# Two first output pairs run together, seven products each, with operand splits in an interleaved queue

## The chip, the core and the metric

The kernel runs on one core of a Trainium2 chip. The metric is the device time of one execution in microseconds. The core has five engines that work side by side, each on a queue of its own in a fixed order: TensorE (PE, with its weight loads PEld), VectorE (DVE), ScalarE (ACT), GpSimd (POOL) and SyncE (SP), which here issues the DMAs. An instruction whose semaphore has not come yet holds up all that stands behind it on its engine.

## The reference

A single decoder layer on 2048 rows of 1024 numbers, in float32. Cut to what matters here:

```python
def mixer_layer(h, norm_g, w_in, conv_w, ret_norm_g, w_out, pos):
    hn = rms_norm(h, norm_g)
    proj = jnp.einsum('bld,de->ble', hn, w_in)
    cx, cb, cc, cg, q, k, v, rg = jnp.split(proj, N_PROJ, axis=-1)
    conv_out = short_conv_branch(cx, cb, cc, conv_w) * jax.nn.silu(cg)
    ...
    ret = head_group_norm(retention_chunkwise(qf, kf, vf), ret_norm_g)
    ret_out = ret.astype(h.dtype) * jax.nn.silu(rg)
    mixed = jnp.concatenate([conv_out, ret_out], axis=-1)
    return h + jnp.einsum('ble,ed->bld', mixed, w_out)
# then: h = rms_norm(h, final_g), and the 2048 rows after the 16 meta rows are returned
```

The change lies in the last projection, `mixed @ w_out` (2048x1024 by 1024x1024), the addition of x and the last norm.

## The kernel before

**A product in three matmuls.** To multiply float32 numbers in a faster format, each operand tile of 128x512 is split into a high part (a cast on ScalarE, tiles `wh`, `mh`) and a low part (source minus high part, on VectorE, tiles `wl`, `ml`), line 112 and 113 of `split`. Three matmuls (low by high, high by low, high by high) then make one product of 128x128 by 128x512.

**Seven products for eight.** A big product is cut into 2x2 blocks. `quad` (matmuls at L241) forms the four result blocks from seven block products, after sums of blocks on both sides: Winograd's scheme. Each block product is 4 tiles by 3 matmuls, 12 in all. `stationary` makes the sums on the side of the weights (the tiles `ra` and `sa`, four sums on GpSimd per quad) and splits seven times, through a ring of three buffers (`RING`): a split into a buffer waits until the product that used it three steps earlier has ended. The moving side is split once and used by many quads. Its seven operands `m[0]` to `m[6]` lie in fixed tiles `mh00` to `mh63` (operand, then tile 0 to 3), with one buffer each, so that operand i of a new matrix can be split only after the last product of the old matrix with operand i. `quad_plain` (L298) makes the same four blocks from eight products without any sums; it needs a moving block 7 (in the tiles of operand 4), and its split weights (four) lie in the tiles of operand 3.

**Order of work.** The input projections and the two kinds of mixer heads come first. Their last piece is a convolution group of two quads. Then come eight output pairs; a pair is two row tiles of 128 rows. The matrix w_out is the moving side: its blocks come by DMA as tiles `w`, its sums, which were made earlier and stored in `sums_w`, as tiles `t`, except for eight tiles that are held in SBUF (`held`). The rows of `mixed` are the weights (`ra`). Before the change, `moving` splits the four blocks, pair 0 runs plainly while the sums are being split, and pairs 1 to 7 run as quads. After a pair's product, `take` adds the bank in PSUM, the copy of another bank (`tc`) and x (`yo`): one addition on GpSimd (for pair 1 on VectorE) and one on VectorE, which reads PSUM; then comes the square sum on ScalarE and a multiplication by `final_g` (`z`, GpSimd), and at the end the scaling by the row's factor.

**What sets the order.** The program is written as a flow of tiles. A scheduler puts the instructions of each engine into a fixed order, from the order in which they are written and its own estimate of their lengths; `tc.issue_after(i)` queues what is traced under it behind instruction i on i's engine.

Of the kernel before, what the change touches and what calls it, by code (L numbers as in the profile page):

```python
# [1 line left out]

# [6 lines left out]
F32 = mybir.dt.float32  # L9
# [69 lines left out]
def hybrid_trunk(ctx: ExitStack, tc: tile.TileContext, t, out: bass.AP, chunk_decay):  # L79
# [21 lines left out]
    def gen(name="g"):  # L101
        return sb.tile([P, HB + 16], F32, name=name, tag="g", bufs=GEN)[:, : 2 + HB]
# [1 line left out]
    def brief(name="b"):  # L104
        return sb.tile([P, HB + 128], F32, name=name, tag="b", bufs=BRIEF)[:, :HB]

    lowered, third, fifth = [None], [None], [None]

    def split(hi, lo, src, scale=None, eng=nc.vector):

        if scale is None:
            nc.scalar.copy(out=hi, in_=src)  # L112
            lowered[0] = eng.tensor_tensor(out=lo, in0=src, in1=hi.bitcast(F32), op=ALU.subtract)  # L113
            return
        nc.scalar.mul(hi, src, scale)
        nc.vector.scalar_tensor_tensor(  # L116
            out=lo, in0=src, scalar=scale, in1=hi.bitcast(F32), op0=ALU.mult, op1=ALU.subtract
        )

    def add(eng, out, a, b):  # L120
        eng.tensor_tensor(out=out, in0=a, in1=b, op=ALU.add)  # L121

    def sub(eng, out, a, b):
        eng.tensor_tensor(out=out, in0=a, in1=b, op=ALU.subtract)  # L124
# [6 lines left out]
            tiles.append(a)  # L131
        return tiles

    summed = [None]

    powered, powers = [], []

    def stationary(blocks):

        a11, a12, a21, a22 = blocks  # L140
        s1 = sb.tile([P, HB], F32, name="sa", tag="ra", bufs=RAW)

        def parts(src):
            hi = sb.tile([P, HB], F32R, name="wh", tag="wh", bufs=RING)
            lo = sb.tile([P, HB], F32R, name="wl", tag="wl", bufs=RING)
            split(hi, lo, src)
            return hi, lo

        w = [parts(a11), parts(a12)]
# [4 lines left out]
        summed[0] = nc.gpsimd.tensor_tensor(out=a12, in0=a12, in1=a11, op=ALU.subtract)  # L154
        w.append(parts(a11))
        third[0] = lowered[0]
        w += [parts(a) for a in (s1, a21)]
        fifth[0] = lowered[0]
        return w + [parts(a) for a in (a12, a22)]

    def operand(i, kt):
        slot = B12 if i == 7 else i
# [9 lines left out]
    def moving(load, scale=None, after={}):  # L172


        m = [[] for _ in range(8)]
        blocks = []
        for j in range(2):
            for half in range(2):
                for kt in range(KH):
                    k = half * KH + kt  # L180
                    blocks.append(load(k, j))
                    parts(m, BLOCK[half][j], kt, blocks[-1], scale(k) if scale else None)
                    after.get((j, k), lambda: None)()
        return m, blocks

    def block_sums(b11, b12, b22, b21, t1, t3, f, g, eng=nc.vector):

# [24 lines left out]

    loaded = [None]

    def prepared(m, src, ns, held={}):

        for n in ns:
            for kt in range(KH):
                a = held.get((n, kt))
                if a is None:  # L220
                    a = gen("t")[:, :HB]
                    loaded[0] = nc.sync.dma_start(a, src[n, kt])
                parts(m, SUMS[n], kt, a)
# [6 lines left out]
    def quad(w, m, take, steps=()):  # L230


        steps = iter(steps)

        def product(i, bank, first):
            (wh, wl) = w[i]
            for kt in range(KH):
                ks = slice(kt * P, (kt + 1) * P)
                mh, ml = m[i][kt]
                for n, (a, b) in enumerate(((wl, mh), (wh, ml), (wh, mh))):  # L240
                    nc.tensor.matmul(  # L241
                        bank, a[:, ks], b, start=first and kt == 0 and n == 0, stop=kt == KH - 1 and n == 2,
                        skip_group_check=not first,
                    )
# [29 lines left out]
        take(1, 0, xb, None)  # L274

    def plain_part(n, load, slot):
        a = sb.tile([P, HB], F32, name="ra", tag="ra", bufs=RAW)
# [256 lines left out]
    def group_plain(g, m, f, meta, first, between, ahead):  # L534
# [28 lines left out]
        cs = []  # L563

        def complete():
            with tc.issue_after(third[0].ins):
# [311 lines left out]
            nc.gpsimd.tensor_copy(out=state[h], in_=states[-1])  # L878
        return blocks

    def output(pair, m, final_g):
        d = mixed[pair // 2]
        loads = [
            lambda a, i=i, k=k: nc.sync.dma_start(a.rearrange("p (k c) -> p k c", k=KH), d[pair % 2, i, k])
# [6 lines left out]
        for i in range(2):  # L891
            for j in range(2):
                y = gen("yo")[:, :HB]
                row = (2 * pair + i) * P
                nc.sync.dma_start(y, x[row : row + P, j * HB : (j + 1) * HB])
                ys[i][j] = y
        last = [None]
        squares = []

# [4 lines left out]
        def take(i, j, pp, c):  # L904
            y = ys[i][j]
            if c is not None:

                with tc.issue_after(fifth[0].ins) if pair == 1 and i + j == 0 else nullcontext():
                    add(nc.vector if pair == 1 else nc.gpsimd, y, y, c)
            junk = sb.tile([P, HB], F32, name="rot", tag="rot", bufs=1)  # L910

            cut = 2 if c is None and pair == SEQ // (2 * P) - 1 else 1
            for n in range(cut):
                cs = slice(n * HB // cut, (n + 1) * HB // cut)
                last[0] = nc.vector.tensor_tensor(out=y[:, cs], in0=pp[:, cs], in1=y[:, cs], op=ALU.add)  # L915
                at = ss[:, i, 2 * n : 2 * n + 1] if i != j and n else ss[:, i, j : j + 1]
                if pair and i + j == 0:
# [10 lines left out]
        if pair == 0:  # L928
            w = plain_parts(loads)
            prepared(m, sums_w, (1, 3))  # L930
            quad_plain(w, m, take)
            prepared(m, sums_w, (0, 2), held)
        else:
            quad(stationary(load_raw(loads)), m, take, (idle, idle, square))
        for i in range(2):
            tot = small.tile([P, 1], F32, name="tot", tag="tot")
            add(nc.vector, tot, ss[:, i, 0:1], ss[:, i, 1:2])
            if cuts[i] > 1:
                add(nc.vector, tot, tot, ss[:, i, 2:3])
            rs = small.tile([P, 1], F32, name="rf", tag="rf")  # L940
            rsqrt_mean(rs, tot)
            row = (2 * pair + i) * P
            for j in range(2):
                cs = slice(j * HB, (j + 1) * HB)
                y = ys[i][j]
                if i == j:
                    nc.scalar.mul(y, y, rs)
                else:
                    with tc.issue_after(last[0].ins):
                        nc.vector.scalar_tensor_tensor(  # L950
                            out=y, in0=y, scalar=rs, in1=final_g[:, cs], op0=ALU.mult, op1=ALU.mult
                        )
                (nc.scalar if i == j and cuts[i] > 1 else nc.sync).dma_start(out[row : row + P, cs], y)

    nc.scalar.dma_start(gain, t["norm1_g"])

# [180 lines left out]
```

## Time and profile before

| | |
|---|---|
| median of 3 runs | 868.76 us (868.29 to 868.82) |
| the profiled execution | 868.98 us |
| its span, first to last instruction | 867.2 us |
| granted TensorE clock | 0.999 |
| busy in the span: PE, PEld | 855.4 us, 705.0 us |
| busy: DVE, ACT, POOL | 719.6 us, 497.9 us, 392.9 us |
| HBM read, written | 90.91 MB, 25.17 MB |

Busy time on PE counts matmuls that overlap in a pipeline: one is shown with some 390 ns, and the next starts about 227 ns after it. So a stretch is read by the starts of the first and the last matmul. The last product of the convolution group ends at 708.7 us of the span, with plain matmuls of pair 0 ahead of it; pair 1 begins at 726.4 us, and the last matmul ends at 860.

### The profile page before, as it was taken

The numbers are of one execution on the slowest core, as the hardware profiler recorded it, in microseconds if no ns is written. First come the engines' busy times: TensorE is split into PE (matmuls) and PEld (weight loads), VectorE is DVE, ScalarE is ACT, GpSimd is POOL, SyncE is SP. The second block draws the span as 40 slices with busy tenths as digits, with TensorE's granted clock in tenths as the row PEclk, the third lists the DMA queues.
The fourth block names the chain that finished last, engine by engine and source line by source line (L and its number), as shares of the span: only waits on it lengthen the run. The fifth ranks groups of instructions, "written<-read, shape, count | busy, mean of one in ns | idle before, by whom it ended". The sixth has DMA issues, their size and how long they took to land.

```text
span 867.2 us, 12698 instructions
## 1 busy us (share of the span) xinstructions
PE 855.4 (99%) x4216; PEld 705.0 (81%) x4216; DVE 719.6 (83%) x1194; ACT 497.9 (57%) x899; POOL 392.9 (45%) x286
## 2 busy tenths in 40 slices
PE   8999999999999999999999999999999999999996
PEld 5878888888787778788888888888888888888885
DVE  6879988889998977989789898988767799867663
ACT  8676557384754654848375757544333465545553
POOL 0662232323145545452242333354646445678773
PEclk9999999999999999999999999999999999999999
DMA  9723335464656633855263746646122594555441
GB/s 334 222 83 98 74 74 149 120 159 134 158 170 175 214 98 97 300 162 146 62 157 122 153 140 122 206 111 217 48 76 80 170 331 135 169 181 159 159 134 73
DMA packets 127218, 129.51 MB, mean 149 GB/s; under 512 B 58352, under 2 KB 75568, under 8 KB 127152
## 3 DMA queue, kind: packets, MB, share of 16 engines
q1 hardware_dynamic: 126576, 128.30, 50.5%
q8 instruction: 33, 0.54, 0.3%
q10 hardware_dynamic: 576, 0.40, 0.1%
q14 instruction: 33, 0.27, 0.1%
HBM read 90.91 MB, written 25.17 MB: 134 GB/s over the span
## 4 chain that ended last, share of the span: by engine, by line
PE 76%; DVE 6%; issue 2%; ACT 1%; DMA 1%; POOL 0%; SPq 0%; POOLq 0%; DVEq 0%
PE pj L241 64%; PE pj L298 5%; PE ms L840 1%; PE ms L829 1%; PE ms L839 1%; PE ms L816 1%; DVE wl L113 1%; PE ms L464 1%; DMA w<-in_w_out 1%; DVE ml L113 0%; DVE qg L869 0%; DVE ml L116 0%; DVE w L124 0%; DVE u L605 0%; DVE tc L605 0%
## 5 line engine op out<-in xcount | busy, mean ns | idle before, releaser
L241 PE MATMUL pj<-mh,wl 128*128 128x512 f32 x1008 | 396.0, 393 | 1.0 <-DVE wl L113 1.0
L241 PE MATMUL pj<-mh,wh 128*128 128x512 f32 x1008 | 393.1, 390 | 0.0
L241 PE MATMUL pj<-ml,wh 128*128 128x512 f32 x1008 | 392.8, 390 | 0.0
L112 ACT CAST wh<-ra 128x512 fp32r<-128x512 f32 x216 | 134.0, 620 | 233.7 <-PE pj L241 195.9
L113 DVE TENSOR_TENSOR wl<-ra,wh 128x512 fp32r<-128x512 f32 x216 | 191.2, 887 | 41.9 <-ACT wh L112 40.9
L241 PEld LDWEIGHTS pj<-mh,wl 128*128 128x128 f32 x1008 | 189.3, 188 | 42.7 <-issue 2.0
L241 PEld LDWEIGHTS pj<-mh,wh 128*128 128x128 f32 x1008 | 189.3, 188 | 39.4
L241 PEld LDWEIGHTS pj<-ml,wh 128*128 128x128 f32 x1008 | 189.3, 188 | 38.2
L121 POOL TENSOR_TENSOR sa<-ra 128x512 f32<-128x512 f32 x36 | 53.1, 1475 | 109.3 <-DVE wl L113 44.5
L124 POOL TENSOR_TENSOR ra<-sa,ra 128x512 f32<-128x512 f32 x36 | 51.6, 1434 | 83.2 <-DVE wl L113 75.2
L124 POOL TENSOR_TENSOR ra<-ra 128x512 f32<-128x512 f32 x36 | 58.0, 1611 | 57.7 <-PE ms L464 48.4
L154 POOL TENSOR_TENSOR ra<-ra 128x512 f32<-128x512 f32 x36 | 61.2, 1701 | 46.6 <-issue 35.2
L248 ACT COPY tc<-pj 128x512 f32<-128x512 f32 x108 | 62.7, 580 | 0.1
L298 PE MATMUL pj<-mh,mh 128*128 128x512 f32 x128 | 50.6, 397 | 2.0 <-ACT mh L1017 1.4
L298 PE MATMUL pj<-mh,ml 128*128 128x512 f32 x128 | 50.1, 391 | 0.6 <-DVE ml L113 0.6
L298 PE MATMUL pj<-ml,mh 128*128 128x512 f32 x128 | 48.1, 393 | 0.0
L852 POOL TENSOR_TENSOR rp<-rs,neg_half 128x4 f32<-128x4 f32 x16 | 19.4, 1213 | 45.9 <-DVE rs L121 45.7
L915 DVE TENSOR_TENSOR yo<-pj,yo 128x512 f32<-128x512 f32 (+1 forms) x33 | 22.0, 671 | 17.2 <-PE pj L241 8.5
L926 POOL TENSOR_TENSOR z<-yo,final_g 128x512 f32<-128x512 f32 x16 | 26.8, 1674 | 18.5 <-DVE yo L915 18.5
L605 POOL TENSOR_TENSOR c<-c,rr 128x512 f32<-128x512 f32 x14 | 24.5, 1747 | 20.8 <-DVE c L646 12.7
L605 POOL TENSOR_TENSOR c<-c,tc 128x512 f32<-128x512 f32 x14 | 24.4, 1741 | 18.4 <-ACT tc L631 18.2
L856 DVE TENSOR_SCALAR pm<-ms,mv,rp 128x128 f32<-128x128 f32 x64 | 21.8, 404 | 11.8 <-POOL rp L852 11.8
(153 smaller groups left out, 1217.3 us busy)
## 6 DMA issues: line engine op xcount, KB each, us to landing
ra<-in_w_in SPq DMA_DIRECT2D x126, 256.0 KB, 2.8
x<-in_xT SPq DMA_DIRECT2D x48, 256.0 KB, 5.0
w<-in_w_out SPq DMA_DIRECT2D x32, 256.0 KB, 4.8
ra<-mixed SPq DMA_DIRECT2D x32, 256.0 KB, 2.7
yo<-in_x SPq DMA_DIRECT2D x32, 256.0 KB, 4.6
ra<-in_x SPq DMA_DIRECT2D x16, 256.0 KB, 3.5
mixed<-c SPq DMA_DIRECT2D x16, 256.0 KB, 2.6
sums_x<-x SPq DMA_DIRECT2D x16, 256.0 KB, 2.7
```

Source lines behind the costliest of these rows:

```text
L112: nc.scalar.copy(out=hi, in_=src)
L113: lowered[0] = eng.tensor_tensor(out=lo, in0=src, in1=hi.bitcast(F32), op=ALU.subtract)
L121: eng.tensor_tensor(out=out, in0=a, in1=b, op=ALU.add)
L124: eng.tensor_tensor(out=out, in0=a, in1=b, op=ALU.subtract)
L154: summed[0] = nc.gpsimd.tensor_tensor(out=a12, in0=a12, in1=a11, op=ALU.subtract)
L241: nc.tensor.matmul(bank, a[:, ks], b, start=first and kt == 0 and n == 0, stop=kt == KH - 1 and n == 2, skip_group_check=not first,)
L248: copied[0] = nc.scalar.copy(out=c, in_=bank)
L298: nc.tensor.matmul(banks[i], a[:, ks], b, start=half + kt + n == 0, stop=half == 1 and kt == KH - 1 and n == 2,)
L605: eng.tensor_tensor(out=out, in0=a, in1=b, op=ALU.mult)
L856: nc.vector.tensor_scalar(out=y[:, cs], in0=o[:, cs], scalar1=mv[:, c, 0:1], scalar2=rp[:, c, :], op0=ALU.subtract, op1=ALU.mult,)
L915: last[0] = nc.vector.tensor_tensor(out=y[:, cs], in0=pp[:, cs], in1=y[:, cs], op=ALU.add)
L926: nc.gpsimd.tensor_tensor(out=ys[i][j], in0=y, in1=final_g[:, j * HB : (j + 1) * HB], op=ALU.mult)
```

## The change

Pair 0 is no longer computed plainly. Pairs 0 and 1 run together in `quads`: product 0 of pair 0, product 0 of pair 1, product 1 of pair 0, and so on, seven each, 14 products of 12 matmuls; they share the moving operands, which are split as the products reach them. Block 7 is no longer loaded and split, and pair 0's four plain weight splits go. For it, pair 0 has seven weight splits and four weight sums on GpSimd. `stationary_in_turn` is a generator that makes one weight split at a time, as a product ends, and sums in place (no `sa` tile). `moving_in_turn` cuts the work on each moving operand into two halves of two tiles; each half is queued, on ScalarE and VectorE, behind the weight split that was made last for one of the two pairs (`queued`). The first three halves are queued behind weight splits 4, 5 and 6 of the last convolution quad. The x rows of both pairs are loaded after the second half of operand 2's splits are written, and the addition of a copied bank is on GpSimd for pair 1 too. Pairs 2 to 7 run as before.

```diff
+    def stationary_in_turn(blocks):
...
+        yield parts(a11)
+        add(nc.gpsimd, a21, a21, a22)
+        sub(nc.gpsimd, a11, a21, a11)
+        yield parts(a12)
+        sub(nc.gpsimd, a12, a12, a11)
+        yield parts(a11)
+        yield parts(a21)
+        sub(nc.gpsimd, a21, a22, a11)
+        yield parts(a21)
+        yield parts(a12)
+        yield parts(a22)
...
+    def moving_in_turn(load, scale, sums):
...
+        first, second = blocks(0, 0), blocks(1, 0)
+        for part, kts, place in ((first, halves[0], 4), (first, halves[1], 5), (second, halves[0], 6)):
+            with queued(splits[0][place]):
+                part(kts)
+        steps = [second] + [lambda kts, n=n: sums(m, n, kts) for n in (1, 0, 2)] + [blocks(1, 1), lambda kts: sums(m, 3, kts)]
+        steps = [[lambda part=part, kts=kts: part(kts) for kts in halves] for part in steps]
+        steps[0].pop(0)
+        return m, steps
...
+    def quads(ws, m, takes, between=()):
...
+        def follow():
+            for ins, step in zip(latest, next(between, ())):
+                with queued(ins):
+                    step()
+            del latest[:]
...
+        for i in range(7):
+            for n, take in enumerate(takes):
+                if i < 2:
+                    banks[n][i] = ps_proj()
+                bank = banks[n][1 if i in (1, 3, 5) else 0]
+                product(n, i, bank, i in (0, 1, 3))
...
+                ws[n][1] = start(ws[n][0])
+            follow()
...
-                with tc.issue_after(fifth[0].ins) if pair == 1 and i + j == 0 else nullcontext():
-                    add(nc.vector if pair == 1 else nc.gpsimd, y, y, c)
+                add(nc.gpsimd, y, y, c)
...
-    m, b = moving(load_w_out)
+    m, in_turn = moving_in_turn(load_w_out, None, lambda m, n, kts: prepared(m, sums_w, (n,), held, kts))
...
-    for pair in range(SEQ // (2 * P)):
-        output(pair, m, final_g)
+    first_pairs = [output(pair, final_g) for pair in range(2)]
...
+    quads(
+        [stationary_in_turn(load_raw(loads)) for loads, *_ in first_pairs], m, [take for _, _, take, *_ in first_pairs],
+        in_turn,
+    )
```

TensorE, where the last convolution quad (bank pj_6918, its operand 6) ends and pair 0 begins. Before, with the plain pair's banks pj_7205 and pj_7206:

```order
L298 MATMUL pj_7206<-mh00_7028,ml32_7142 128x512
L298 MATMUL pj_7206<-ml00_7029,mh32_7141 128x512
L298 MATMUL pj_7206<-mh01_7034,mh32_7141 128x512
L298 MATMUL pj_7206<-mh01_7034,ml32_7142 128x512
L241 MATMUL pj_6918<-mh60_3953,wl_6915 128x512
L241 MATMUL pj_6918<-ml60_3954,wh_6914 128x512
```

Now, at the border between product 0 of pair 1 (bank pj_7123) and product 1 of pair 0 (pj_7184):

```order
L356 MATMUL pj_7123<-mh03_7046,wl_7087 128x512
L356 MATMUL pj_7123<-ml03_7047,wh_7086 128x512
L356 MATMUL pj_7123<-mh03_7046,wh_7086 128x512
L356 MATMUL pj_7184<-mh10_7052,wl_7120 128x512
L356 MATMUL pj_7184<-ml10_7053,wh_7119 128x512
L356 MATMUL pj_7184<-mh10_7052,wh_7119 128x512
```

The plain matmuls were mixed into the convolution quad; the new products stand whole, one after the other, all behind the quad.

VectorE in the middle of the first pairs, before (`tc` and `c` belong to the convolution group, `wl` to pair 1, `yo` to a take of pair 0):

```order
L113 TENSOR_TENSOR ml23_7178<-t_7175,mh23_7177 128x512
L113 TENSOR_TENSOR ml60_7184<-t_7181,mh60_7183 128x512
L113 TENSOR_TENSOR ml61_7190<-t_7187,mh61_7189 128x512
L113 TENSOR_TENSOR ml62_7196<-t_7193,mh62_7195 128x512
L113 TENSOR_TENSOR ml63_7202<-t_7199,mh63_7201 128x512
L915 TENSOR_TENSOR yo_7125<-pj_7205,yo_7125 128x512
L113 TENSOR_TENSOR wl_7404<-ra_7382,wh_7403 128x512
```

and now:

```order
L113 TENSOR_TENSOR wl_7263<-ra_7070,wh_7262 128x512
L113 TENSOR_TENSOR ml40_7285<-held_6722,mh40_7284 128x512
L113 TENSOR_TENSOR ml41_7289<-held_6722,mh41_7288 128x512
L113 TENSOR_TENSOR wl_7281<-ra_7078,wh_7280 128x512
L113 TENSOR_TENSOR ml42_7293<-held_6723,mh42_7292 128x512
L113 TENSOR_TENSOR ml43_7297<-held_6723,mh43_7296 128x512
L113 TENSOR_TENSOR wl_7316<-ra_7070,wh_7315 128x512
L113 TENSOR_TENSOR ml50_7341<-w_7338,mh50_7340 128x512
```

The splits of the moving operands no longer come in long rows ahead of pair 1: a weight split now stands ahead of every two of them.

GpSimd at the same place, before:

```order
L605 TENSOR_TENSOR c_6873<-c_6873,rr_2923 128x512
L121 TENSOR_TENSOR sa_7390<-ra_7386,ra_7388 128x512
L124 TENSOR_TENSOR ra_7386<-ra_7382,ra_7386 128x512
L605 TENSOR_TENSOR c_6873<-c_6873,tc_6960 128x512
L124 TENSOR_TENSOR ra_7382<-sa_7390,ra_7382 128x512
L154 TENSOR_TENSOR ra_7384<-ra_7384,ra_7382 128x512
L926 TENSOR_TENSOR z_7258<-yo_7125,final_g_7122 128x512
```

and now:

```order
L718 TENSOR_TENSOR c_6873<-c_6873,rr_2923 128x512
L121 TENSOR_TENSOR ra_7078<-ra_7078,ra_7080 128x512
L124 TENSOR_TENSOR ra_7068<-ra_7068,ra_7066 128x512
L718 TENSOR_TENSOR c_6873<-c_6873,tc_6960 128x512
L124 TENSOR_TENSOR ra_7074<-ra_7078,ra_7074 128x512
L121 TENSOR_TENSOR yo_7168<-yo_7168,tc_7115 128x512
L121 TENSOR_TENSOR yo_7176<-yo_7176,tc_7136 128x512
L124 TENSOR_TENSOR ra_7076<-ra_7076,ra_7074 128x512
L1041 TENSOR_TENSOR z_7201<-yo_7168,final_g_7062 128x512
```

The sums of two pairs (ra_7066 to 7072 and ra_7074 to 7080) and the additions of copied banks (`yo<-yo,tc`) now stand between the convolution group's last operations and the first `z`.

SyncE's DMA queue around the last w_out operands, before (tiles `yo` are rows of x, `ra` are weights, `t` are stored sums):

```order
L435 DMA w_7116<-in_w_out 128x512
L895 DMA yo_7125<-in_x 128x512
L895 DMA yo_7127<-in_x 128x512
L895 DMA yo_7129<-in_x 128x512
L895 DMA yo_7131<-in_x 128x512
L884 DMA ra_7151<-mixed0_89 128x512
L222 DMA t_7157<-sums_w_88 128x512
```

and now, around the sums of operand 6 (t_7406 to t_7424):

```order
L997 DMA ra_7551<-mixed1_90 128x512
L997 DMA ra_7553<-mixed1_90 128x512
L997 DMA ra_7555<-mixed1_90 128x512
L997 DMA ra_7731<-mixed1_90 128x512
L273 DMA t_7406<-sums_w_88 128x512
L273 DMA t_7412<-sums_w_88 128x512
L273 DMA t_7418<-sums_w_88 128x512
```

The stored sums of operand 6 have moved behind weight loads of pairs 2 and 3.

More of the change, by code (lines that the diff above doesn't have):

```diff
@@ L1 @@
[L1 removed]
+from contextlib import ExitStack, contextmanager, nullcontext
 import concourse.bass as bass
@@ L132, in load_raw, with queued @@
         return tiles
-    summed = [None]
+    summed, splits = [None], [None]
+    @contextmanager
+    def queued(instructions):
+        with ExitStack() as order:
+            for ins in instructions:
+                order.enter_context(tc.issue_after(ins.ins))
+            yield
     powered, powers = [], []
@@ L213, in hybrid_trunk, with prepared @@
     loaded = [None]
-    def prepared(m, src, ns, held={}):
+    def prepared(m, src, ns, held={}, kts=range(KH)):
         for n in ns:
-            for kt in range(KH):
+            for kt in kts:
                 a = held.get((n, kt))
@@ L565, in complete @@
         def complete():
-            with tc.issue_after(third[0].ins):
+            with queued(splits[0][2][1:]):
                 for j in range(2):
@@ L890, in output, with fetch @@
         cuts = [1, 1]
[L891 to L896, printed above, removed]
+        def fetch():
+            for i in range(2):
+                for j in range(2):
+                    y = gen("yo")[:, :HB]
+                    row = (2 * pair + i) * P
+                    nc.sync.dma_start(y, x[row : row + P, j * HB : (j + 1) * HB])
+                    ys[i][j] = y
         last = [None]
@@ L926, in take @@
                 nc.gpsimd.tensor_tensor(out=ys[i][j], in0=y, in1=final_g[:, j * HB : (j + 1) * HB], op=ALU.mult)
[L928 to L953, printed above, removed]
@@ new lines, in finish @@
+        def finish():
+            for i in range(2):
+                tot = small.tile([P, 1], F32, name="tot", tag="tot")
+                add(nc.vector, tot, ss[:, i, 0:1], ss[:, i, 1:2])
+                if cuts[i] > 1:
+                    add(nc.vector, tot, tot, ss[:, i, 2:3])
+                rs = small.tile([P, 1], F32, name="rf", tag="rf")
+                rsqrt_mean(rs, tot)
+                row = (2 * pair + i) * P
+                for j in range(2):
+                    cs = slice(j * HB, (j + 1) * HB)
+                    y = ys[i][j]
+                    if i == j:
+                        nc.scalar.mul(y, y, rs)
+                    else:
+                        with tc.issue_after(last[0].ins):
+                            nc.vector.scalar_tensor_tensor(
+                                out=y, in0=y, scalar=rs, in1=final_g[:, cs], op0=ALU.mult, op1=ALU.mult
+                            )
+                    (nc.scalar if i == j and cuts[i] > 1 else nc.sync).dma_start(out[row : row + P, cs], y)
@@ L955, in hybrid_trunk @@
+        return loads, fetch, take, square, finish
     nc.scalar.dma_start(gain, t["norm1_g"])
```

84 lines of the change are left out of this document (73 added, 11 removed).

## The prediction

> **What bounds the kernel now.** I read the page's head first, then the chain of work that ended last, then the stretch where the change lies (689 to 746 us), engine by engine. From the page and the chain (start, length, engine, tile, line, count):
>
> ```profile
> span 867.2 us, 12698 instructions
> PE 855.4 (99%) x4216; PEld 705.0 (81%) x4216; DVE 719.6 (83%) x1194; ACT 497.9 (57%) x899; POOL 392.9 (45%) x286
> ...
> 705.99 2.72 PE pj L241 x12
> 708.71 17.68 PE pj L298 x78
> 726.38 133.58 PE pj L241 x588
> 859.99 0.76 DVE yo L915 x2
> ```
>
> TensorE is busy for 99% of the span. The last row of the chain before the tail is 588 matmuls on end: seven pairs of 84, 133.58 / 588 = 0.2272 us each, no wait named. Whatever ends the first pair earlier or later moves the end of the kernel by the same amount. A product of 12 matmuls is 2.72 us.
>
> TensorE's own rows at the place where the first pair begins, with the idle time before a row and its releaser in brackets:
>
> ```profile
> 698.53 0.61 PE L298 MATMUL pj<-mh,mh 128*128 128x512 f32 x2
> 699.35 0.50 PE L298 MATMUL pj<-mh,ml 128*128 128x512 f32 x1 [0.20 <-DVE ml L113]
> ```
>
> At 698.53 product 4 of the last convolution quad has ended, and the first plain matmuls start. From there to 726.38 stand 120 matmuls: the quad's products 5 and 6 (24) and the plain pair (96). At 2.72 us for 12 they need 27.2 of the 27.85 us. So TensorE is almost never short of operands here. What feeds it, over the stretch in which VectorE makes those operands (length, then busy us and count of PE, PEld, DVE, ACT, POOL, clock, DMA share, GB/s), and beside it a later stretch:
>
> ```profile
> 689.68:731.13 41.45, 41.25 (x182) 33.86 (x181) 41.11 (x55) 28.67 (x56) 19.38 (x10) 1.00 0.72 257
> 740.00:780.00 40.00, 40.00 (x176) 32.78 (x176) 29.23 (x38) 20.03 (x41) 29.51 (x23) 1.00 0.58 179
> ```
>
> VectorE has no room: 41.11 of 41.45 us, with ten GpSimd operations beside it. (One of its 55 began earlier; 54 start inside.) ScalarE has a third free. Later, VectorE is at 73%. How VectorE and GpSimd stand to each other, row by row:
>
> ```profile
> 707.98 1.30 POOL L121 TENSOR_TENSOR sa<-ra 128x512 f32<-128x512 f32 x1 [1.00 <-DMA ra<-mixed]
> 709.37 1.62 POOL L124 TENSOR_TENSOR ra<-ra 128x512 f32<-128x512 f32 x1
> ...
> 708.05 0.68 DVE L121 TENSOR_TENSOR tc<-pj,tc 128x512 f32<-128x512 f32 x1
> 708.66 1.18 DVE L113 TENSOR_TENSOR ml<-w,mh 128x512 fp32r<-128x512 f32 x1
> 709.76 1.77 DVE L113 TENSOR_TENSOR ml<-t,mh 128x512 fp32r<-128x512 f32 x1
> 711.45 0.68 DVE L113 TENSOR_TENSOR ml<-w,mh 128x512 fp32r<-128x512 f32 x1
> 712.06 0.68 DVE L113 TENSOR_TENSOR wl<-ra,wh 128x512 fp32r<-128x512 f32 x1
> 712.66 0.68 DVE L605 TENSOR_TENSOR tc<-tc,rr 128x512 f32<-128x512 f32 x1
> ```
>
> With GpSimd quiet, VectorE starts a subtract every 0.60 us (712.06, 712.66) and shows 0.68. Beside a GpSimd operation the subtract shows 1.77, that is 1.09 more. If the GpSimd operation started while VectorE read PSUM (tc<-pj at 708.05 kept its 0.68), only 0.50 is lost (1.18). The whole stretch: 54 x 0.60 = 32.4, and 41.45 - 32.4 = 9.05 for ten GpSimd operations and one wait,
>
> ```profile
> 724.61 3.10 DVE L113 TENSOR_TENSOR ml<-held,mh 128x512 fp32r<-128x512 f32 x5 [0.24 <-ACT mh L112]
> ```
>
> so (9.05 - 0.24) / 10 = 0.88 us of VectorE for each GpSimd operation.
>
> **The change part by part.** I call the products of the two first pairs A0 to A6 and B0 to B6; they run A0, B0, A1, B1 and so on.
>
> *Matmuls.* Pair 0 goes from 96 to 84, the order of all engines is the same up to this place, and the other six pairs keep theirs. If TensorE never waited, A0 would start at 698.53 + 24 matmuls (5.44) = 703.97, and 168 matmuls at 0.2267 would end at 742.06. Before, pair 2 began at 726.38 + 84 x 0.2272 = 745.46. The most there is to gain is 3.4 us: 2.7 of the 12 matmuls, the rest the small losses that the plain products had.
>
> *Splits.* Block 7 (4 splits) and the four plain weight splits go; 14 weight splits come in place of those 4 and of pair 1's 7. Every split costs VectorE 0.60. What matters is how many must be made by when. Before, one split moving tile served 6 plain matmuls; now it serves 6 again, but each product needs a new weight pair as well, and only three weight buffers are there, so a weight split starts when the product three back has ended. Such a step by itself fits: the last quad's product 0 ends four products before 698.53, at 687.65, and its cast and subtract follow,
>
> ```profile
> 687.90 0.62 ACT L112 CAST wh<-sa 128x512 fp32r<-128x512 f32 x1 [0.58 <-PE pj L241]
> 689.68 0.69 DVE L113 TENSOR_TENSOR wl<-sa,wh 128x512 fp32r<-128x512 f32 x1
> ```
>
> With 0.25 from matmul to cast, 0.62 and 0.69, this is about 1.6 us in a free queue, under two products (5.44 us) of cover. The cover is gone when VectorE's queue is late. ScalarE is no limit: about 58 operations between 690 and 737, at 28.67 / 56 = 0.51 us each 30 us.
>
> *VectorE and GpSimd up to A5.* I count the new order from wl<-sa of the last quad (it stands where the row at 689.68 stands) to the subtract of A5's weights: 48 VectorE operations. GpSimd has 18 large operations that are due in that stretch, from c<-c,rr to the second yo<-yo,tc of product 2; before, it had ten in a stretch nearly as long. The eight more are the weight sums of a second pair and four additions, which now go to GpSimd for both pairs (`add(nc.gpsimd, y, y, c)`). Price of one: 0.50 at the least, 1.09 at the most by the rows; 0.88 on average before, where four of ten came during a PSUM read. There are six such reads among the 48, seven among the 54, so I take four cheap ones again, of 18: 4 x 0.50 + 14 x 1.09 = 17.26. Sum: 48 x 0.60 = 28.80, + 17.26 + 0.24 of waits = 46.30; 689.68 + 46.30 = 735.98.
>
> When is it due? A5 is 12 products after 698.53: 698.53 + 12 x 2.72 = 731.17. So A5 starts about 4.8 us late. The lateness builds up over products 2 to 4, where GpSimd has no gap. From A5 four product times remain (A5, B5, and A6 with B6): 735.98 + 10.88 = 746.86.
>
> The Trainium skill, "SBUF — State Buffer", section "Who interferes with whom", says that a VectorE instruction with two SBUF inputs and a GpSimd instruction that reads SBUF exclude each other for a whole instruction, and that one with at most one SBUF input is not touched. The second half is the 0.68 at 708.05. By the first, each GpSimd operation would cost its own 1.30 us, and the sum would be 48 x 0.60 + 18 x 1.30 + 0.24 = 52.4; the rows say 1.09 and less, and I stay with them.
>
> *The last operand's loads.* The four t tiles of product 6 are now queued on SP behind five ra loads; each of these waits for a weight split to free its buffer, the last for B5's (wl, two VectorE rows after A5's, about 737.2). Issues, waits and landings of these kinds before:
>
> ```profile
> SPq L884 <- DVE wl L113: 22.8, 10, 6.2
> ra<-mixed SPq DMA_DIRECT2D x19, 256.0 KB, 2.7
> t<-sums_w SPq DMA_DIRECT2D x8, 256.0 KB, 5.4
> 703.18 4.69 SPq L222 DMA_DIRECT2D t<-sums_w x6
> ```
>
> First t issued at about 738.6 (two issues at 0.65 to 0.78), landed 2.7 to 5.4 later, split 1.4 after: 742.7 to 745.4. Product 6 is due at 735.98 + 5.44 = 741.4. I take 0.6, little above the least, since queues were full when the 5.4 was taken (16 w loads on end) and are not here: bounds 0 and 4. The loads of block 5 stand behind the two mixed stores, which wait for c (GpSimd, about 712); they land by 720 and are due at 731, so they cost nothing.
>
> *Other edits.* The x rows are fetched earlier or as early, four w loads (1 MB) go: nothing, DMA share 0.72 before. At the boundary to pair 2, the cast of its second weight waits for the end of A6, with two takes and a scaling ahead of its subtract (0.6 + 0.75 + 0.6 + 0.69 and the cast's lag against 2.72): 0 to 0.7, taken as nothing.
>
> **Sum.** 746.86 + 0.6 = 747.5 against 745.46: 2.0 us more. The profiled execution took 868.98 (span 867.2), so it would be 871.0; the median of the runs is 0.2 lower, 868.76, so I forecast 870.8. With price p for a GpSimd operation the difference is 18p - 15.3 or so: no change at p = 0.85, the floor (-3.4) below 0.69.
>
> **Rivals.** *A: hidden.* GpSimd's operations fall into VectorE's waits for PSUM and casts, p is under 0.7 and A5 is in time. For it: in the later stretch above, 23 GpSimd operations and 38 of VectorE live in 40 us and PE is full. Against it: VectorE waits for almost nothing in 689 to 731. Time 868.76 - 3.4 = 865.4. It decides if p stays under 0.75 (18p - 15.3 = -1.8).
>
> *B: full alternation.* If GpSimd always has its next operation ready, the two take turns, as they do here:
>
> ```profile
> 715.06 6.38 DVE L113 TENSOR_TENSOR ml<-t,mh 128x512 fp32r<-128x512 f32 x6
> 714.08 1.62 POOL L605 TENSOR_TENSOR c<-c,tc 128x512 f32<-128x512 f32 x1 [3.10 <-ACT tc L631]
> 715.66 1.74 POOL L124 TENSOR_TENSOR ra<-sa,ra 128x512 f32<-128x512 f32 x1
> 717.48 1.62 POOL L154 TENSOR_TENSOR ra<-ra 128x512 f32<-128x512 f32 x1
> ```
>
> and then VectorE waits for GpSimd too (the take of product 1 needs yo<-yo,tc). All 18 at 1.09, two more of them ahead of A5 (the additions of product 3) and 1 us of waits: 18p grows to 20 x 1.09 + 1 = 22.8, 5.5 us over my 17.26: 876. The skill's whole-instruction rule, named above, would give 18 x 1.30 = 23.4, about the same time.
>
> *C: loads alone.* VectorE is in time, but the t tiles land 5.4 us after their issue. In-time B5 splits end at about 730, the fifth ra load is issued at 730.1, the first t at 730.8, split by 737.6, due at 736.6; with the other three behind other transfers up to 3 us are lost: about 868.3, no change.
>
> **Chances.** My forecast (weights 2.3 to 7 us late at A5, 868.3 to 873.0): 0.52, of which 0.18 within 0.2% (1.74 us, about what a measurement of this kernel can tell from no change) and 0.34 slower. A 0.26, faster. B 0.12, slower. C 0.10, same. So faster 0.26, same 0.28, slower 0.46. The range runs from A's time to p = 1.09 with 2 us of load waits (18 x 1.09 - 15.3 + 1.4 = 5.7): 865.4 to 874.5.
>
> **What would show it.** Right: in the changed profile VectorE is busy above 95% from 700 to 735, the chain of waits passes from PE to DVE wl L113 between products 2 and 5, PE waits for wl in 4 to 6 us there, GpSimd is above 70%. Wrong: PE full to 742, then the 12 matmuls are simply won (A); or PE's waits are for ACT mh or DMA t at product 6 alone (C).

## The result: 0.8% slower, and the profile after

The changed kernel took 875.82 us (median of 4 runs, 875.38 to 875.95) against 868.79 (868.29 to 869.08) for the kernel before beside it: a ratio of 1.0076, 95% interval 1.0064 to 1.0088, so 7.0 us more. The forecast was 870.8 with a range up to 874.5. The direction was right and the size was not; the time is that of rival B, 876, which had been given a chance of 0.12 (how far B's reasons hold is told below). The profiled execution took 875.38.

The head of its page:

```profile
span 873.6 us, 12673 instructions
PE 856.4 (98%) x4204; PEld 703.8 (81%) x4204; DVE 732.4 (84%) x1190; ACT 498.7 (57%) x901; POOL 407.7 (47%) x296
```

TensorE ran 12 matmuls fewer (4204), VectorE four operations fewer (1190), and yet VectorE is busy 12.8 us longer and GpSimd 14.8 us longer. Over the whole span that looks harmless (84% and 47%). The stretch of the two pairs does not. Here it is from wl<-sa of the last quad (689.19) to the point where VectorE is done with A5's weights; behind the length stand busy time and instructions of PE, PEld, DVE, ACT and POOL, then clock, DMA share and GB/s:

```profile
689.19:738.22 49.03, 43.51 (x179) 34.11 (x178) 48.70 (x49) 27.95 (x53) 34.84 (x20) 0.97 0.48 170
```

VectorE is busy in 48.70 of 49.03 us with 49 operations (48 start inside), one per us where one alone takes 0.60. GpSimd runs 20 operations in 34.84 us, 1.74 each where one alone takes 1.30. What stood among them, by groups of GpSimd's instructions in this stretch:

```profile
L124 POOL TENSOR_TENSOR ra<-ra 128x512 f32<-128x512 f32 x6 | 11.3, 1886 | 5.6 <-issue 4.3 <-ACT tc L363 0.7 <-DVE wl L113 0.6
L121 POOL TENSOR_TENSOR yo<-yo,tc 128x512 f32<-128x512 f32 x6 | 10.1, 1703 | 0.1
L718 POOL TENSOR_TENSOR c<-c,rr 128x512 f32<-128x512 f32 x2 | 4.1, 2048 | 2.0 <-DVE c L642 2.0
L718 POOL TENSOR_TENSOR c<-c,tc 128x512 f32<-128x512 f32 x2 | 3.4, 1708 | 0.0
L121 POOL TENSOR_TENSOR ra<-ra 128x512 f32<-128x512 f32 x2 | 3.4, 1685 | 1.9 <-DMA ra<-mixed 1.9
L1041 POOL TENSOR_TENSOR z<-yo,final_g 128x512 f32<-128x512 f32 x2 | 3.3, 1672 | 3.7 <-DVE yo L1030 3.7
```

All six additions and all eight weight sums lie ahead of A5's weights. Read in order of time, the two engines take turns; VectorE first, then GpSimd:

```profile
707.86 1.79 DVE L113 TENSOR_TENSOR ml<-t,mh 128x512 fp32r<-128x512 f32 x1
709.56 1.78 DVE L113 TENSOR_TENSOR wl<-ra,wh 128x512 fp32r<-128x512 f32 x1
711.27 3.48 DVE L113 TENSOR_TENSOR ml<-t,mh 128x512 fp32r<-128x512 f32 x2
714.67 1.74 DVE L113 TENSOR_TENSOR wl<-ra,wh 128x512 fp32r<-128x512 f32 x1
```

```profile
709.06 1.74 POOL L718 TENSOR_TENSOR c<-c,tc 128x512 f32<-128x512 f32 x1
710.76 1.74 POOL L124 TENSOR_TENSOR ra<-ra 128x512 f32<-128x512 f32 x1
712.46 3.41 POOL L121 TENSOR_TENSOR yo<-yo,tc 128x512 f32<-128x512 f32 x2
715.83 1.73 POOL L124 TENSOR_TENSOR ra<-ra 128x512 f32<-128x512 f32 x1
```

Each engine starts an operation every 1.70 us. A pair of operations, one of each, costs VectorE 1.70 where its own costs 0.60: 1.1 us for the one of GpSimd.

VectorE was not waiting for results of GpSimd in the meantime. From 689 to 738 its only wait is the second of these two rows (us in total, times, the longest); the first falls into pair 2, at 767:

```profile
DVE yo L1030 <- POOL yo L121: 1.2, 1, 1.2
DVE tc L121 <- PE pj L292: 0.3, 1, 0.3
```

TensorE pays. What it waited for between 700 and 770 us (us in total, times, the longest), and the single waits in its timeline, in brackets, for A2, B2, A3 and B3:

```profile
PE pj L356 <- DVE wl L113: 5.5, 5, 2.0
PE pj L356 <- DVE ml L113: 0.5, 1, 0.5
PE pj L292 <- DVE yo L1030: 0.4, 1, 0.4
```

```profile
716.47 0.50 PE L356 MATMUL pj<-mh,wl 128*128 128x512 f32 x1 [1.95 <-DVE wl L113]
719.97 0.50 PE L356 MATMUL pj<-mh,wl 128*128 128x512 f32 x1 [0.48 <-DVE wl L113]
723.48 0.50 PE L356 MATMUL pj<-mh,wl 128*128 128x512 f32 x1 [0.46 <-DVE wl L113]
728.55 0.50 PE L356 MATMUL pj<-mh,wl 128*128 128x512 f32 x1 [2.02 <-DVE wl L113]
```

A wait costs a little more than the row says: the matmul after it shows 0.50 where others show 0.39, and the next one starts 0.34 after it (716.47, 716.81) and not 0.23. By the starts of the products, each against the one before it plus 2.72 us, the losses are 2.11 at A2, 0.78 at B2, 0.80 at A3, 2.35 at B3, 1.57 at A4, 0.98 at B4, 0.13 at A5, and 0.77 in product 6: 9.5 us. A0 starts at 703.48, so that pair 2 could begin at 741.57 and begins at 751.05; before it was 745.55. Pair 2 then takes 19.70 in place of 19.04: ahead of its last product, at 767.88, TensorE waits for a take (yo), and that take had waited 1.2 us for an addition on GpSimd, which is the first row of VectorE's waits above (0.66 more). The border itself, from 750.82 to 751.05, is one matmul's step and costs nothing. The 4.0 us that were to be had became 6.2 us of loss; with 0.2 in the rest this is the 6.4 by which the span grew.

The 1.57 at A4 is no wait. TensorE ran at half its clock there, after the longest wait:

```profile
727.00:729.00 2.00, 0.45 (x2) 0.40 (x3) 2.00 (x2) 1.44 (x3) 1.37 (x2) 1.00 0.36 131
729.00:731.00 2.00, 2.00 (x8) 1.59 (x7) 2.00 (x3) 0.72 (x2) 2.00 (x2) 0.69 0.03 8
731.00:733.00 2.00, 2.00 (x6) 1.47 (x6) 2.00 (x2) 0.94 (x2) 2.00 (x2) 0.50 0.37 131
733.00:735.00 2.00, 2.00 (x10) 1.64 (x9) 2.00 (x2) 1.11 (x2) 1.88 (x2) 0.96 0.45 135
```

Was this stretch a cause of its own? The chain of work that ended last goes from VectorE over it and back to VectorE:

```profile
726.75 1.76 DVE wl L113
728.55 3.66 PE pj L356 x10
732.41 3.48 DVE ml L113 x2
735.89 0.61 DVE wl L113
736.55 5.75 PE pj L356 x24
```

B4's weights (735.89) come from a queue of VectorE that is behind by itself, so I read the half clock as hidden; one run below tests it.

### The profile page after: what moved, and what is told of

It is laid out like the page before. It is cut to its first block, busy times and chain, and to the rows that moved or that the text cites. A ratio compares the mean times of both kernels' runs of the same rounds, so it can differ in the third digit from the quotient of the medians.

```text
span 873.6 us, 12673 instructions
## 1 busy us (share of the span) xinstructions
PE 856.4 (98%) x4204; PEld 703.8 (81%) x4204; DVE 732.4 (84%) x1190; ACT 498.7 (57%) x901; POOL 407.7 (47%) x296
## 4 chain that ended last, share of the span: by engine, by line
PE 72%; DVE 8%; issue 3%; POOL 1%; DMA 1%; ACT 0%; SPq 0%; POOLq 0%; DVEq 0%
PE pj L292 61%; PE pj L411 2%; DVE ml L113 2%; DVE wl L113 2%; PE pj L356 2%; PE ms L953 1%; PE ms L942 1%; PE ms L952 1%; PE ms L929 1%; PE ms L577 1%; DMA w<-in_w_out 1%; DMA t<-sums_w 1%; DVE ml L116 0%; DVE yo L1030 0%; POOL yo L121 0%
## 5 line engine op out<-in xcount | busy, mean ns | idle before, releaser
L292 PE MATMUL pj<-mh,wl 128*128 128x512 f32 x980 | 385.1, 393 | 1.2 <-DVE wl L113 0.8
L292 PE MATMUL pj<-mh,wh 128*128 128x512 f32 x980 | 382.2, 390 | 0.0
L292 PE MATMUL pj<-ml,wh 128*128 128x512 f32 x980 | 381.9, 390 | 0.0
L113 DVE TENSOR_TENSOR wl<-ra,wh 128x512 fp32r<-128x512 f32 x224 | 205.7, 921 | 38.2 <-ACT wh L112 35.5
L124 POOL TENSOR_TENSOR ra<-ra 128x512 f32<-128x512 f32 x41 | 68.5, 1670 | 63.4 <-PE ms L577 48.8
L163 POOL TENSOR_TENSOR ra<-ra 128x512 f32<-128x512 f32 x35 | 60.1, 1716 | 49.5 <-issue 38.2
L411 PE MATMUL pj<-mh,mh 128*128 128x512 f32 x96 | 38.9, 406 | 0.5 <-ACT mh L115 0.5
L411 PE MATMUL pj<-mh,ml 128*128 128x512 f32 x96 | 37.5, 391 | 1.0 <-DVE ml L113 1.0
L121 POOL TENSOR_TENSOR yo<-yo,tc 128x512 f32<-128x512 f32 x24 | 36.7, 1540 | 2.7 <-ACT tc L299 2.4
L411 PE MATMUL pj<-ml,mh 128*128 128x512 f32 x96 | 35.8, 393 | 0.0
L121 DVE TENSOR_TENSOR tc<-pj,tc 128x512 f32<-128x512 f32 x28 | 19.2, 686 | 14.4 <-PE pj L292 14.3
```

The source lines that it names most:

```text
L113: parted[1] = eng.tensor_tensor(out=lo, in0=src, in1=hi.bitcast(F32), op=ALU.subtract)
L292: nc.tensor.matmul(bank, a[:, ks], b, start=first and kt == 0 and n == 0, stop=kt == KH - 1 and n == 2, skip_group_check=not first,)
L411: nc.tensor.matmul(banks[i], a[:, ks], b, start=half + kt + n == 0, stop=half == 1 and kt == KH - 1 and n == 2,)
```

## The experiments

My theory: VectorE's operations with two SBUF inputs and GpSimd's operations cannot run at once; with GpSimd at work for 71% of the stretch, each of its 20 operations costs VectorE about 1.0 us, and VectorE's lateness sets TensorE's products 2 to 4. Rivals: VectorE simply has too many operations; or the chain through the rings of buffers (cast, subtract, sum) is too long whatever the engines do. All times are medians, and each ratio is to runs of the kernel before on the same chip. That kernel took 868.70 to 868.94 on the chips used, so times from different chips compare to within some 0.3 us.

**The work on GpSimd made short.** The eight weight sums and six additions of pairs 0 and 1 work on 16 of 512 columns and leave the other 496 out; nothing else is changed:

```
-        add(nc.gpsimd, a21, a21, a22)
+        add(nc.gpsimd, a21[:, :W], a21[:, :W], a22[:, :W])
...
-                add(nc.gpsimd, y, y, c)
+                    add(nc.gpsimd, y[:, :W], y[:, :W], c[:, :W])
```

> The eight weight sums and six additions of pairs 0 and 1 on GpSimd work on 16 of their 512 columns, so that most of that work is left out; the order of every engine is the changed kernel's, row by row. Theory: 14 of the 20 GpSimd operations in the stretch cost VectorE 0.2 instead of 1.0; 48 x 0.60 + 6 x 1.0 + 14 x 0.2 = 37.6 us, less than the 41.5 that are there until A5 is due, TensorE does not wait, 865.4 to 866.5 us, and no stretch at half clock. Rival 1: VectorE's rows are the same, so no change, 875 us. Rival 2: waits stay at 3 to 5 us, 872 to 875 us. Rival 3 (TensorE's half clock is a loss of its own, whatever the waits): 867.5 us.

Measured: 865.69 us (865.37 to 866.83), ratio 0.9965 (0.9952 to 0.9978). The same 49 us of the span:

```profile
689.20:738.20 49.00, 49.00 (x218) 40.58 (x217) 42.24 (x63) 34.81 (x69) 24.22 (x25) 1.00 0.66 224
```

TensorE is full, and VectorE does 63 operations in the time of 49. The edit changes no order, no buffer and no number of instructions (VectorE runs 1190 in both). So neither the count on VectorE nor the rings cost the 10 us: the length of GpSimd's operations did.

**The weight sums on VectorE.** The same eight sums with `nc.vector` in place of `nc.gpsimd`:

> The eight weight sums of pairs 0 and 1 move from GpSimd to VectorE; all else as in the changed kernel (875.8 us). Theory (VectorE and GpSimd exclude each other, a GpSimd operation takes about 1.0 us of VectorE's time, the same operation on VectorE 0.60): 8 x 0.4 = 3.2 us less, 872.5 us, TensorE's waits for wl fall from 5.5 to 2 or 3 us. Rival 1 (VectorE merely has too many operations of its own): 8 x 0.60 = 4.8 us more, 880 us. Rival 2 (the chain product end, cast, subtract through three weight buffers is too long): no change, 875 to 876 us.

Measured: 871.59 us (871.32 to 872.2), ratio 1.0031 (1.0019 to 1.0044). VectorE has eight operations more and the kernel is 4.2 us faster than the changed one, against 8 x (0.99 - 0.60) = 3.1 by the theory; the two profiled spans differ by 3.2 (873.6 and 870.4). TensorE waits 3.4 us for wl, in two waits, where 2 to 3 were expected. A too large number of VectorE operations would have made it slower.

**The additions on VectorE, from PSUM.** ScalarE's copies of the banks and GpSimd's additions of them are replaced by VectorE additions that read the bank itself:

```
-                    copies[n] = copy(bank)
+                    take(0, 0, bank, None, True)
...
+            if partly:
+                add(nc.vector, y, pp, y)
+                return
```

> For pairs 0 and 1 the copies of a bank on ScalarE and the additions of the copies on GpSimd (six) go; VectorE adds the bank to x straight from PSUM instead (six more operations that read PSUM). The x rows are fetched two steps earlier for it. Theory: six GpSimd operations less (6.0 us of VectorE's time), six of 0.60 more (3.6): 2.4 us less, more if GpSimd's own lateness also counts, 872 to 873.4 us. Rival 1: 3.6 us more, 879 us. Rival 2: no change.

Measured: 871.44 us (871.01 to 872.33), ratio 1.0028 (1.0016 to 1.0040): 4.4 us under the changed kernel for six operations moved. This is 0.6 below the range that I expected, and the theory's sum had 2.4. The profiled spans differ by 3.1 (873.6 and 870.5); what gave the rest is not shown.

**The same additions on VectorE, from the copies in SBUF.** `add(nc.vector if pair < 2 else nc.gpsimd, y, y, c)`, nothing else:

> The changed kernel with the additions of a copied bank on VectorE, which still read the copy in SBUF and y in SBUF: as many VectorE operations as the run in which these additions read PSUM directly (871.44), but each with two SBUF inputs, and ScalarE's copies stay. My theory (what costs is two operations with SBUF inputs on the two engines at one time): six GpSimd operations go, which is 6 x (1.0 - 0.6) = 2.4 less than the changed kernel, 873.4, at best 872; so 0.6 to 2.0 slower than with PSUM read directly, where these six also stand beside GpSimd freely. Rival (the source of the operand doesn't matter, only the count on each engine): 871.2 to 871.7, the same as with PSUM.

Measured: 872.88 us (872.02 to 873.4), ratio 1.0051 (1.0036 to 1.0066). This lies where the theory put it, but its interval meets that of the run from PSUM, so the two times by themselves do not settle it. Nor do the two kernels differ in the source alone: the one that reads PSUM has no copies on ScalarE and loads x earlier. VectorE's rows say more, though they are few. In both runs five of the six additions fall where GpSimd has nothing to do and take 0.67 or 0.68 us, from PSUM or not. One stands beside a GpSimd operation. From PSUM, VectorE and then GpSimd:

```profile
710.19 0.68 DVE L121 TENSOR_TENSOR yo<-pj,yo 128x512 f32<-128x512 f32 x1
709.67 1.75 POOL L718 TENSOR_TENSOR c<-c,tc 128x512 f32<-128x512 f32 x1
```

From the copies:

```profile
710.71 1.78 DVE L121 TENSOR_TENSOR yo<-yo,tc 128x512 f32<-128x512 f32 x1
710.20 1.74 POOL L718 TENSOR_TENSOR c<-c,tc 128x512 f32<-128x512 f32 x1
```

With both inputs in SBUF the addition takes 1.78, from PSUM 0.68. VectorE's other PSUM reads beside GpSimd agree: 0.68 at 708.05 in the kernel before, 0.67 at 702.14 and 0.68 at 705.55 in the changed one. The GpSimd operation is not free even so: the VectorE operation behind each of these reads takes 1.18 or 1.19, about 0.5 more than alone. The two runs do not show that a read of PSUM helps the operations behind it further: all 28 subtracts from 703 to 738 us take 28.0 us in the one and in the other.

The Trainium skill, "SBUF — State Buffer", section "Who interferes with whom", says that a VectorE instruction with two SBUF inputs shuts out a GpSimd instruction that reads SBUF and the reverse, and that one with at most one SBUF input does not contend. These rows agree with both halves. Its whole-instruction lock would make each GpSimd operation cost its own 1.30 us; the turns here cost 1.1, and 0.99 on the mean of 20.

**Both edits.** The sums on VectorE and the additions from PSUM:

> The changed kernel with both earlier edits (the weight sums on VectorE, and the additions on VectorE straight from PSUM), but with the products of z left on GpSimd, unlike the fastest run (866.23), which had those in VectorE's scaling too. My theory: fourteen GpSimd operations fewer; the six multiplications that stay cost 0.4 us each more than in the fastest run where they fall before A5, but TensorE had slack there by then: 866.0 to 867.5. Rival (the gain of the fastest run came from the fused scaling): 868.5 to 869.5, what the two edits give if their gains overlap.

Measured: 868.49 us (867.66 to 869.84, 10 runs), ratio 0.9998 (0.9989 to 1.0007): the rival's number, not mine. TensorE still waited 1.0 us for wl, 0.7 for ml and 0.3 for yo. The place, in VectorE's and GpSimd's timelines:

```profile
718.53 0.68 DVE L1033 TENSOR_TENSOR yo<-pj,yo 128x512 f32<-128x512 f32 x1
719.13 1.19 DVE L113 TENSOR_TENSOR wl<-ra,wh 128x512 fp32r<-128x512 f32 x1
720.24 2.38 DVE L113 TENSOR_TENSOR ml<-held,mh 128x512 fp32r<-128x512 f32 x2
722.54 0.68 DVE L121 TENSOR_TENSOR yo<-pj,yo 128x512 f32<-128x512 f32 x1
```

```profile
716.88 4.59 POOL L1044 TENSOR_TENSOR z<-yo,final_g 128x512 f32<-128x512 f32 x2 [8.45 <-DVE yo L1033]
```

Two products z = yo * final_g cost VectorE 1.6 us (1.19 + 2.38 beside 0.68 + 1.28). I had expected slack in TensorE there; VectorE had none. Whether these two operations or the order around them made the loss, the next run asked.

**Both edits, the z products short.** Four GpSimd instructions work on 16 of 512 columns, and ScalarE's scaling reads yo in place of z, so that these blocks lack the gain final_g. The order on every compute engine is that of the run above:

```
-                nc.gpsimd.tensor_tensor(out=ys[i][j], in0=y, in1=final_g[:, j * HB : (j + 1) * HB], op=ALU.mult)
+                nc.gpsimd.tensor_tensor(out=ys[i][j][:, :w], in0=y[:, :w], in1=final_g[:, cs], op=ALU.mult)
```

> The kernel with both edits that still had the products z = yo * final_g on GpSimd (868.49), with these four products cut to 16 of 512 columns (ScalarE's scaling reads yo instead, so the gain final_g is left out of these blocks). The order on every engine stays as it was. My theory (GpSimd's operations with SBUF inputs hold up VectorE, and VectorE had no slack at products 2 and 3): the two products that stood at 716.88 to 721.47 cost VectorE about 1.6 us (its rows of 1.19 and 2.38 beside 0.68 and 1.28), two more stood at 734.55 to 739.2; with them short TensorE's waits for wl (1.0 us) and their restarts go and the wait for ml (0.7) shrinks: 866.2 to 867.2, as with the scaling fused. Rival (the fused scaling gained 2.3 us by another order of the splits and scalings around pair 2, and the products are innocent): 868.0 to 868.8.

Measured: 866.18 us (865.56 to 866.92), ratio 0.9967 (0.9954 to 0.9979). The rows at the same place:

```profile
718.61 0.67 DVE L114 TENSOR_TENSOR wl<-ra,wh 128x512 fp32r<-128x512 f32 x1
719.20 1.28 DVE L114 TENSOR_TENSOR ml<-held,mh 128x512 fp32r<-128x512 f32 x2
```

TensorE has no wait for wl or ml left. Four GpSimd instructions in a stretch of 50 us were worth 2.3 us; the order was not.

**Everything on VectorE.** Both edits, and the products of z fused into VectorE's scaling (`scalar_tensor_tensor` with rs and final_g, as the other blocks have it) for the first two pairs:

> For pairs 0 and 1: weight sums on VectorE, banks added straight from PSUM on VectorE, and the multiplication by final_g fused with the row scaling on VectorE at the end (as the other half of the blocks has it), so that GpSimd has only the convolution group's four operations in the stretch. Theory: 62 VectorE operations x 0.60 + 4 x 1.0 + 0.5 = 41.7 us against 41.5: TensorE waits under 1 us before A5, 865.5 to 867.5 us, below the kernel before (868.8). Rival 1: 14 more operations, 8.4 us more, 884 us. Rival 2: 872 to 876 us.

Measured: 866.23 us (865.26 to 867.2), ratio 0.9971 (0.9959 to 0.9983). This is faster than the kernel before, by 2.7 us, and than the changed one by 9.6. VectorE has 77 operations in the stretch, 28 more than in the changed kernel, in no more time:

```profile
689.20:738.20 49.00, 49.00 (x218) 40.48 (x217) 48.31 (x77) 30.92 (x60) 13.18 (x7) 1.00 0.66 230
```

**The z products alone.** The fused scaling in the changed kernel, sums and additions left on GpSimd:

> The changed kernel with only the products of z fused into VectorE's scaling for the first two pairs; the weight sums and additions stay on GpSimd. Two GpSimd operations of twenty go ahead of A5's weights, and the splits of product 6 and the scalings stand in another order around pair 2. My theory: 2 x 0.985 less up to A5, and up to 0.6 less at the border to pair 2, where a take waits behind a product of GpSimd: 873.0 to 874.3. Rival (GpSimd's remaining operations run ahead into the place of the two, and cost VectorE as much a little earlier): 875.2 to 876.

Measured: 872.40 us (872.32 to 874.51), ratio 1.0046 (1.0031 to 1.0062), 3.4 under the changed kernel and 0.6 under what I had expected at best. In the profiled span it is 3.1: A5 comes at 737.61 where it came at 739.40 (1.8, about the price of two operations), and the waits for ml and, in pair 2, for yo are gone. They had cost 0.77 and 0.66; of the latter about half comes back, since pair 2 still takes 19.38 us with another pause at 759.6, whose cause is not shown.

**The order of the splits.** Each operand queued whole behind pair 0's weights, not in halves:

```
-            for ins, step in zip(latest, next(between, ())):
-                with queued(ins):
+            for step in next(between, ()):
+                with queued(latest[0]):
```

> The changed kernel with each operand's splits queued whole behind the splits of pair 0's weights, not in two halves. Same instructions, other order on VectorE and ScalarE. My theory: the sum of VectorE's work with GpSimd's between sets the end, order little: 875 to 877, with single waits at TensorE that are longer at pair 1's products (their weights stand behind four splits instead of two). Rival (the order in halves is what loses the time, because it makes the casts and subtracts wait for each other): 870 to 873.

Measured: 876.87 us (876.18 to 877.57), ratio 1.0096 (1.0079 to 1.0113). As expected: three waits for wl of 7.0 us together in place of five of 5.5, and VectorE as full (48.66 of 49 us, 49 operations beside GpSimd's 20). The queueing in halves is not what lost the time.

**The half clock taken away.** Seven spare matmuls right behind A3, while TensorE would wait for B3's weights:

```
+                if (n, i) == (0, 3):
+                    with tc.issue_after(last_mm[0].ins):
+                        warm_up(FILL)
```

> The changed kernel with seven spare bf16 matmuls (into a bank that nothing reads) right behind product A3, where TensorE waited 2.35 us for B3's weights and then ran at a granted clock of 0.50 for 3.41 us. My theory (VectorE and GpSimd exclude each other, the lateness is theirs): the half clock lay under VectorE's lateness, since B4's weights came at 735.8 to 736.5 whatever TensorE did; the stretch at half clock goes, and the time stays at 875.0 to 875.9 (0 to 0.8 under the changed kernel). Rival (the half clock is on the path that sets the end): half of 3.41 us comes back, 1.6 to 2.0, 873.8 to 874.2.

Measured: 876.12 us (875.14 to 876.65), ratio 1.0088 (1.0073 to 1.0103), no faster than the changed kernel and 0.2 above what I had expected. The granted clock where it had been 0.69 and 0.50:

```profile
729.00:731.00 2.00, 1.99 (x9) 1.65 (x10) 2.00 (x2) 0.26 (x1) 1.96 (x2) 1.00 0.00 0
731.00:733.00 2.00, 1.03 (x5) 0.53 (x3) 2.00 (x3) 2.00 (x5) 2.00 (x2) 1.00 0.33 127
```

TensorE ran at full clock and then waited 0.98 us for A4's weights and 0.97 for B4's instead. Pair 2 begins 47.6 us after A0, and did so in the changed kernel (751.53 - 703.93, 751.05 - 703.48). The half clock was a consequence that cost nothing here.

## Why the prediction failed

- **The floor was right.** The forecast had 3.4 us as the most to gain, 865.4. With GpSimd out of the way the runs gave 865.69, 866.18 and 866.23, which is 3.3, 2.5 and 2.7 under the kernel before on the same chips.
- **The place and the signs were right.** VectorE above 95% from 700 to 735 (9.00 of 9.00 us, stretch after stretch), the chain passing from PE to wl between products 2 and 5, 5.5 us of waits for wl where 4 to 6 were named, GpSimd at 71% of the stretch.
- **The term that was mis-sized: GpSimd's operations ahead of A5.** I took 18 of them for 17.26 us, as 4 at 0.50 and 14 at 1.09. There were 20: the additions of product 3 came ahead as well, as rival B had it. The 49.03 us, less 48 x 0.60 and 0.3 of waits, leave 19.9 for 20, so 0.99 each. VectorE was through at 738.22 in place of 735.98, 2.2 us later, although it had started 0.5 earlier. The average of the kernel before, 0.88, was the price while GpSimd had gaps. In the changed kernel it was busy for 8.54 of the 9 us from 707 to 716 and 8.24 of the 9 from 725 to 734. By the starts of VectorE's rows only two of the 20 were cheap, behind PSUM reads (702.74 and 706.15, 0.50 each), where I had taken four; sixteen cost 1.1, one 0.97, and the first, under way when the stretch began, 0.1.
- **A step that was missing: B4.** The sum followed VectorE's queue to one deadline, A5, and then let TensorE run. But A5 started at 739.40, 1.2 us after its weights, since B4 had waited until 736.55 and takes 2.72 us. Lateness at an earlier product that no later one makes up has to be carried along.
- **The loads** of the last operand were taken at 0.6 and cost 0.77. That this was near is luck: by the sum's own times, 742.7 against 741.4, the least was 1.3, and product 6 began at 744.84, 3.4 us later than forecast.
- **Pair 2.** The border to it, taken as nothing within 0 to 0.7, cost nothing. The 0.66 was lost inside pair 2, where a take waited for GpSimd; the forecast had no term for that.

Together 2.2 + 1.2 + 0.2 + 0.7 is 4.3 of the 4.4 us between the 871.0 for a profiled execution and its 875.38. The upper end of the range was built with 18 operations at 1.09 and 2 us of load waits; it left out that the number and the waits behind it move with the price. So rival B deserved more than 0.12: the rows of turns at 1.6 to 1.7 us that spoke for it were in the prediction, and so was its condition, GpSimd with no gap over products 2 to 4. That its time came out is luck in part. B had 22.8 us for GpSimd's operations and for VectorE's waits on them, where the runs showed 19.9 and no such wait ahead of A5, and it had neither the step at B4 nor the loss in pair 2.

## What to carry to other kernels

Where VectorE is full, an elementwise operation given to GpSimd is not free: here it cost VectorE 1.0 us on the mean, and 0.5 where it began beside a VectorE operation that reads PSUM, against 0.60 for doing it on VectorE. So in such a stretch fold the work into VectorE, straight from PSUM where it can be, and leave GpSimd the stretches where VectorE has gaps. For a forecast, follow the lateness from product to product to the one that carries it to the end, and price a shared resource by its rows under full load, not by its average.

## What the chip showed that I had not expected

- **Half clock after a short wait.** The granted clock fell to 0.50 after a TensorE wait of 2.02 us in the changed kernel, of 2.23 with the sums on VectorE and of 2.97 with whole operands, for about 3.4 us each: from the rows above (1 - 0.69) / 0.5 x 2, + 2, + (1 - 0.96) / 0.5 x 2 is 3.4, and in the two other runs a window of 9 us shows 0.81. It did not after waits up to 1.95, and once not after 2.25 (whole operands, before 738.78). The Trainium skill, "TensorE: Matmul & The Clock Gate", Part 1, gives a free-running window of 3.4 us, which agrees with the length and with a threshold that is not sharp; its table under "Why this matters for your kernels" warns of idle gaps above about 3 us, and here 2.0 were enough. In the run with the sums on VectorE no wait follows the stretch, so it may have cost up to 1.6 us there; that was not tried.
- **GpSimd can be the one that waits.** With the z products short, one on only 16 columns took 1.80 us on GpSimd beside a VectorE without a gap (0.22 later, beside gaps), and held up no VectorE row that I could see. It ended at 718.16, just after VectorE's next PSUM read began (718.00), and a second one likewise (720.57, 720.41). Why GpSimd got no turn between VectorE's operations here, as it did in the changed kernel, is open.

```profile
716.36 1.80 POOL L1049 TENSOR_TENSOR z<-yo,final_g 128x16 f32<-128x16 f32 x1 [8.45 <-DVE yo L1036]
734.31 0.22 POOL L1049 TENSOR_TENSOR z<-yo,final_g 128x16 f32<-128x16 f32 x1
```
